# A block-wise seven-product matmul in a float32 decoder layer: another order of the products, other transfers for the weight sums of the last quarter, and one multiply on another engine

## The chip, the cores and the metric

The kernel runs on one core of one Trainium2 chip. The metric is the device time of one execution in microseconds (us). Three runs of the kernel before are shown with a median of 873.74 us.

## What is computed

The reference is one layer of a decoder trunk over 512 tokens of width 1024, in float32: an RMSNorm, one wide input projection, three token mixers (a gated recurrence, dilated attention, attention into a memory), their gated sum through `w_out`, and then an MLP and a last RMSNorm. The change lies in these last lines alone:

```python
    hm = _rmsnorm(x, g_mlp)
    x = x + jnp.square(jax.nn.relu(hm @ w_mlp_in)) @ w_mlp_out    # 1024 -> 4096 -> 1024
return _rmsnorm(x, g_final)
```

## The kernel before

TensorE has no float32 product of full accuracy here, so each float32 operand is split into a rounded part and a rest: `hi = round(src)` on ScalarE (`whi`, `shi`) and `lo = src - hi` on VectorE (`wlo`, `slo`), and a product is three matmuls, hi·hi, hi·lo and lo·hi. A matmul here has 128x128 stationary and 512 moving columns.

**The MLP** runs in four quarters of 1024 hidden columns each. `in_part` computes 128 hidden columns of a quarter (24 matmuls, lines 200 to 202, `mm3`), `hidden` squares their relu into `sq`. The second MLP product of a quarter, 512 x 1024 x 1024, is done by `Product7`: activations and weights are taken as 2x2 blocks (a11 to a22, b11 to b22) and seven products p1 to p7 of block sums replace eight. A weight block is 512x512 floats, 1 MB, in a tile `wq` (one buffer per block, tags `wq00` to `wq11`). `STEPS` gives the order of the seven products, for each the PSUM bank (x, y or z), whether it opens the bank, which quarter of the residual `x2` the bank is then added to, and the sign. In the order before, p1, p2, p5, p6, p7, p4, p3, each product is two parts of 12 matmuls (lines 1118 to 1120): `prep` makes the sums of blocks, `stationary` splits the activation, `split` splits one half of the weight block, `multiply` issues the matmuls and `add` adds the bank to `x2` on VectorE.

**Order of the work.** The list `parts` strings the products and the `in_part`s of the next quarter together; quarters 0 to 2 have `in_part`s between their products, the last quarter (q = 3) has none. The last loop multiplies part i and then splits part i+4, so splits run four parts ahead (four buffers each of `whi` and `wlo`). Within that, each engine has one queue that is worked off in order; the tile framework sets the final order.

**Weight sums.** p5, p6, p7 and p4 take sums of weight blocks (b11+b12, b11+b12+b22 and b12+b22, and all four). In quarters 0 to 2 VectorE adds them in place (128x2048, `V.tensor_add` in `prep`). In the last quarter (`queue` true) they are made by accumulating transfers (`accumulate`: a DMA from GpSimd's queue that adds w_mlp_out's block onto a tile), into `wq01`, `wq00` and a third tile `t2` (`load_sum`, in a `raw` buffer); t2 is used by p6 and, after one more block was added to it, by p4. `free` issues the loads of the next quarter's blocks when a product no longer needs the buffer (`FREE`), on SyncE's queue; `LOADS` is their order for the first quarter.

**The end.** `add` calls `final` for p2, p7, p4 and p3, with which a 128x512 half of `x2` is complete. The first half of a token tile: ScalarE sums its squares, GpSimd multiplies it by `g_final` (line 1157). The second half: ScalarE squares it into the output tile `hnx` (two buffers), VectorE adds the sums, GpSimd raises to the power -0.5 (`rsf`), ScalarE and VectorE scale the two halves, and SyncE sends them out (lines 1171, 1174). A third tile thus needs the buffer of the first, which is free when both of its transfers have landed. The last product is cut for token tile e = 1 into two pieces of 256 columns.

Of the kernel before, what the change touches and what calls it, by code (L numbers as in the profile page):

```python
# [17 lines left out]
P = 128  # L18
# [121 lines left out]
def hybrid_block(ctx: ExitStack, tc: tile.TileContext, x, mem, g_mix, w_in, b_gate, conv_w, conv_b,  # L140
# [856 lines left out]
    class Product7:  # L997
# [14 lines left out]
        def load(self, kh, nh):  # L1012
            b = self.b[kh, nh] = ml.tile([P, 4, 512], F32, name="wq", tag=f"wq{kh}{nh}")
            nc.sync.dma_start(b, self.block(kh, nh))
            if self.queue and (kh, nh) == (0, 1):
                self.accumulate(b, 1, 1)
# [4 lines left out]
        def load_sum(self):  # L1021

            self.t2 = raw_tile(4, 512)
            nc.sync.dma_start(self.t2, self.block(0, 0))
            self.accumulate(self.t2, 0, 1)
            self.accumulate(self.t2, 1, 1)
# [17 lines left out]
        def prep(self, p, sq):  # L1044
# [8 lines left out]
            if p == 5:  # L1053
                self.u = self.sums()
                V.tensor_sub(self.u, a21, a22)
                if not self.queue:
                    V.tensor_add(b11, b11, b12)
# [14 lines left out]
            elif p == 4:  # L1072
                if self.queue:
                    b11 = self.t2
                else:
                    V.tensor_add(b11, b11, b21)
                act, w = a22, b11
            elif p == 3:
                V.tensor_add(self.u, self.u, a12)
                act, w = self.u, b22  # L1080
            else:
                act, w = a12, b21
# [4 lines left out]
        STEPS = ((1, "x", True, (0, 0), 1), (2, "y", True, (0, 0), 1), (5, "z", True, (1, 1), 1),  # L1087
                 (6, "x", False, (0, 1), -1), (7, "x", False, (1, 1), -1), (4, "x", False, (1, 0), 1),
                 (3, "z", False, (0, 1), 1))

        def parts(self, n, sq, done, free):
# [6 lines left out]
            def split(kh):  # L1098
# [4 lines left out]
                if kh == 1:  # L1103
                    free(p)
                    if self.queue and p == 1:
                        self.accumulate(self.b[0, 0], 0, 1)
                    if self.queue and p == 6:
                        self.accumulate(self.t2, 1, 0)
# [40 lines left out]
    def final(t, nh, c0, c1):  # L1149

        v = x2[t][:, nh * 512 + c0:nh * 512 + c1]
        if t not in ss0:
# [4 lines left out]
            G.tensor_tensor(v, v, gbf[:, nh * 512:(nh + 1) * 512], op=ALU.mult)  # L1157
# [37 lines left out]
    def in_part(q, n):  # L1195
        now = {}

        def split():
            m, e = q * 4 + n // 2, n % 2
            now["w"] = split_w(raws[m][:, :, e * P:(e + 1) * P], KT, P)  # L1200
            if e == 1:
                load_in(m + 2)
                if m == 14:
                    prods[3].load_sum()
# [10 lines left out]
    LOADS = ((0, 0), (1, 0), (0, 1), (1, 1))  # L1215
# [4 lines left out]
    for q in range(4):  # L1220
        def free(p, q=q):
            for b in FREE.get(p, ()) if q < 3 else ():
                prods[q + 1].load(*b)
# [50 lines left out]
```

## Time and profile before

| | |
|---|---|
| median of 3 runs (lowest, highest) | 873.74 us (873.71, 875.11) |
| the profiled execution: its time, its span | 873.91 us, 872.1 us |
| TensorE busy | 852.6 us, 98% of the span |
| VectorE, ScalarE, GpSimd busy | 546.9 us (63%), 388.2 us (45%), 31.9 us (4%) |
| mean granted TensorE clock | 0.994 of full speed |

The sum of the prediction is made against the profiled execution, whose time is 0.17 us above the median; 1.8 us of it lie outside the span. A wait is idle time of an engine put down to what released it. Times in the timeline are us from the start of the span. The last quarter begins at about 817 us.

### The profile page before, as it was taken

The page shows a single profiled execution, that of the slowest core. Times are in us where ns is not written, and L with a number is a line of the kernel's source. Part 1 is how long each engine was busy: PE and PEld are TensorE (multiplying, and loading weights), DVE is VectorE, ACT ScalarE, POOL GpSimd, SP SyncE. Part 2 cuts the span into 40 slices and gives each one's busy share as a digit, 9 for nine tenths or more (in the row PEclk, how much of TensorE's full clock was granted, in tenths as well). Part 3 has the DMA queues.
Part 4 walks back from the last instruction along what each step waited for, and adds up shares of the span by engine and source line. Part 5 has one row for each costly group of instructions (what it writes and reads, how often), then busy time and mean ns, then how long its engine had stood idle before and what let it go on. Part 6 is the DMA issues. An engine that isn't in the chain of part 4 may idle for free.

```text
span 872.1 us, 10543 instructions
## 1 busy us (share of the span) xinstructions
PE 852.6 (98%) x4275; PEld 714.6 (82%) x4275; DVE 546.9 (63%) x695; ACT 388.2 (45%) x586; POOL 31.9 (4%) x39
## 2 busy tenths in 40 slices
PE   8999999999999999999999999999999999999975
PEld 7789888889888888888888889888888888888864
DVE  5787766754679642542524446488669757866685
ACT  5467656754635522332332234344425434344444
POOL 2010000000000000000000000000000000001022
PEclk9999999999999999999999999999999999999989
DMA  8862233334322132242325426412431442229422
GB/s 247 265 205 77 68 97 97 97 103 140 114 87 91 49 121 72 82 136 73 101 73 193 141 96 222 141 49 95 147 96 49 145 145 69 76 96 230 108 49 97
DMA packets 82332, 101.16 MB, mean 116 GB/s; under 512 B 3707, under 2 KB 64199, under 8 KB 82156
## 3 DMA queue, kind: packets, MB, share of 16 engines
q1 hardware_dynamic: 78316, 89.03, 32.1%
q0 software_dynamic: 3696, 10.77, 5.4%
q8 instruction: 33, 0.54, 0.3%
q10 hardware_dynamic: 272, 0.69, 0.2%
q14 instruction: 15, 0.12, 0.0%
HBM read 97.32 MB, written 5.52 MB: 118 GB/s over the span
## 4 chain that ended last, share of the span: by engine, by line
PE 85%; DVE 6%; DMA 4%; ACT 2%; issue 2%; POOL 0%; SPq 0%; POOLq 0%; ACTq 0%
PE ps L200 18%; PE ps L202 18%; PE ps L201 18%; PE ps L1118 4%; PE ps L1119 4%; PE ps L1120 4%; DMA wq<-in_w_mlp_out_dram 2%; DVE wlo L95 2%; PE ps L954 2%; PE ps L953 2%; PE ps L952 2%; PE ps L526 1%; PE ps L527 1%; PE ps L528 1%; DMA raw<-in_w_in_dram 1%
## 5 line engine op out<-in xcount | busy, mean ns | idle before, releaser
L95 DVE TENSOR_TENSOR wlo<-raw,whi 128x1024 fp32r<-128x1024 f32 (+1 forms) x125 | 147.7, 1187 | 151.9 <-ACT whi L95 147.6
L95 ACT ACTIVATE whi<-raw 128x1024 fp32r<-128x1024 f32 (+1 forms) x126 | 129.8, 1032 | 222.4 <-PE ps L201 163.6
L200 PE MATMUL ps<-hT_hi,whi 128*128 128x512 f32 x400 | 156.8, 392 | 0.1
L202 PE MATMUL ps<-hT_hi,wlo 128*128 128x512 f32 x400 | 155.6, 390 | 0.4 <-DVE wlo L95 0.4
L201 PE MATMUL ps<-hT_lo,whi 128*128 128x512 f32 x400 | 155.8, 390 | 0.0
L95 DVE TENSOR_TENSOR wlo<-wq,whi 128x1024 fp32r<-128x1024 f32 x52 | 65.4, 1258 | 59.7 <-ACT whi L95 59.7
L95 ACT ACTIVATE whi<-wq 128x1024 fp32r<-128x1024 f32 x52 | 55.0, 1060 | 102.5 <-PE ps L201 51.3
L1118 PE MATMUL ps<-whi,shi 128*128 128x512 f32 (+1 forms) x228 | 89.2, 391 | 5.8 <-DVE x L95 5.8
L201 PE MATMUL ps<-hmT_lo,whi 128*128 128x512 f32 x240 | 93.4, 389 | 0.0
L202 PE MATMUL ps<-hmT_hi,wlo 128*128 128x512 f32 x240 | 93.4, 389 | 0.0
L200 PE MATMUL ps<-hmT_hi,whi 128*128 128x512 f32 x240 | 93.2, 389 | 0.0
L1119 PE MATMUL ps<-wlo,shi 128*128 128x512 f32 (+1 forms) x228 | 88.8, 390 | 0.0
L200 PEld LDWEIGHTS ps<-hT_hi,whi 128*128 128x128 f32 x400 | 75.1, 188 | 16.7 <-issue 0.6
L202 PEld LDWEIGHTS ps<-hT_hi,wlo 128*128 128x128 f32 x400 | 75.1, 188 | 16.4 <-DVE wlo L95 0.8
L1120 PE MATMUL ps<-whi,slo 128*128 128x512 f32 (+1 forms) x228 | 88.4, 388 | 0.0
L201 PEld LDWEIGHTS ps<-hT_lo,whi 128*128 128x128 f32 x400 | 75.1, 188 | 15.1
L1118 PEld LDWEIGHTS ps<-whi,shi 128*128 128x128 f32 x228 | 43.5, 191 | 15.8 <-issue 4.9
L202 PEld LDWEIGHTS ps<-hmT_hi,wlo 128*128 128x128 f32 x240 | 45.1, 188 | 9.4
L201 PEld LDWEIGHTS ps<-hmT_lo,whi 128*128 128x128 f32 x240 | 45.1, 188 | 9.2
L200 PEld LDWEIGHTS ps<-hmT_hi,whi 128*128 128x128 f32 x240 | 45.0, 188 | 9.3
L1120 PEld LDWEIGHTS ps<-whi,slo 128*128 128x128 f32 x228 | 43.3, 190 | 8.8
L1119 PEld LDWEIGHTS ps<-wlo,shi 128*128 128x128 f32 x228 | 43.4, 190 | 8.6
(253 smaller groups left out, 1344.0 us busy)
## 6 DMA issues: line engine op xcount, KB each, us to landing
raw<-in_w_in_dram SPq DMA_DIRECT2D x23, 1024.0 KB, 5.4
raw<-in_w_mlp_in_dram SPq DMA_DIRECT2D x16, 1024.0 KB, 5.8
wq<-in_w_mlp_out_dram SPq DMA_DIRECT2D x16, 1024.0 KB, 6.8
raw<-in_w_in_dram SPq DMA_DIRECT2D x12, 512.0 KB, 5.2
raw<-in_w_mem_kv_dram SPq DMA_DIRECT2D x4, 1024.0 KB, 5.2
raw<-in_w_out_dram SPq DMA_DIRECT2D x4, 1024.0 KB, 5.0
x<-in_x_dram SPq DMA_DIRECT2D x7, 512.0 KB, 4.3
raw<-in_w_lru_out_dram SPq DMA_DIRECT2D x4, 768.0 KB, 4.5
```

The source lines that it names most:

```text
L95: r = fn(*a, **k)
L200: PE.matmul(ps, whi[:, k0 + k, :], ah, start=k == 0, stop=False)
L201: PE.matmul(ps, whi[:, k0 + k, :], al, start=False, stop=False)
L202: PE.matmul(ps, wlo[:, k0 + k, :], ah, start=False, stop=k == nk - 1)
L526: PE.matmul(ps[:, 0:256], ah, hi[:, k % 4, :], start=k == 0, stop=False)
L527: PE.matmul(ps[:, 0:256], ah, lo[:, k % 4, :], start=False, stop=False)
L952: PE.matmul(ps, ah[:, sl], hi[:, k % 2, :], start=k == 0, stop=False)
L953: PE.matmul(ps, ah[:, sl], lo[:, k % 2, :], start=False, stop=False)
L954: PE.matmul(ps, al[:, sl], hi[:, k % 2, :], start=False, stop=k == KT - 1)
L1118: PE.matmul(o, ah[:, k, sl], hi, start=opens and k == 0, stop=False, **more)
L1119: PE.matmul(o, ah[:, k, sl], lo, start=False, stop=False, **more)
L1120: PE.matmul(o, al[:, k, sl], hi, start=False, stop=k == 3, **more)
```

## The change

It changes five things. (1) `STEPS`: the products are done in the order p1, p5, p6, p2, p7, p3, p4, in all four quarters, and `LOADS` follows. (2) In the last quarter b11+b12 for p5 is added by VectorE as in the others; b11 lies in a `raw` buffer that is loaded earlier. (3) The sum of three for p6 (`t2`) is made in a buffer of the `sq` tiles, which is free when p7 of the third quarter is split (`load_sum3`: one load, two accumulating transfers). (4) The sum of four for p4 (`t4`) is made in `wq00` by a copy of t2 from SBUF to SBUF on GpSimd's queue and one accumulating transfer (`load_sum4`); b12+b22 for p7 is accumulated in `wq01` after VectorE has read b12. (5) The multiply by `g_final` goes from GpSimd to VectorE.

```diff
--- before.py
+++ after.py
@@ -1009,21 +1009,24 @@
 
             return cols(self.w, nh * 512, 512, self.k0 + kh * 4, 4)
 
-        def load(self, kh, nh):
-            b = self.b[kh, nh] = ml.tile([P, 4, 512], F32, name="wq", tag=f"wq{kh}{nh}")
+        def load(self, kh, nh, dst=None):
+            b = self.b[kh, nh] = dst or ml.tile([P, 4, 512], F32, name="wq", tag=f"wq{kh}{nh}")
             nc.sync.dma_start(b, self.block(kh, nh))
-            if self.queue and (kh, nh) == (0, 1):
-                self.accumulate(b, 1, 1)
 
         def accumulate(self, dst, kh, nh):
             nc.gpsimd.dma_start(out=dst, in_=self.block(kh, nh), accum_op=ALU.add)
 
-        def load_sum(self):
-
-            self.t2 = raw_tile(4, 512)
-            nc.sync.dma_start(self.t2, self.block(0, 0))
-            self.accumulate(self.t2, 0, 1)
-            self.accumulate(self.t2, 1, 1)
+        def load_sum3(self, dst):
+
+            self.t2 = dst
+            nc.sync.dma_start(dst, self.block(0, 0))
+            self.accumulate(dst, 0, 1)
+            self.accumulate(dst, 1, 1)
+
+        def load_sum4(self):
+            self.t4 = ml.tile([P, 4, 512], F32, name="wq", tag="wq00")
+            nc.gpsimd.dma_start(self.t4, self.t2)
+            self.accumulate(self.t4, 1, 0)
 
         def stationary(self, src):
             i, self.n = self.n, self.n + 1
@@ -1053,8 +1056,9 @@
             if p == 5:
                 self.u = self.sums()
                 V.tensor_sub(self.u, a21, a22)
-                if not self.queue:
-                    V.tensor_add(b11, b11, b12)
+                V.tensor_add(b11, b11, b12)
+                if self.queue:
+                    self.accumulate(b12, 1, 1)
                 act, w = self.u, b11
             elif p == 6:
                 u, self.u = self.u, self.sums()
@@ -1071,7 +1075,7 @@
                 act, w = a11, b12
             elif p == 4:
                 if self.queue:
-                    b11 = self.t2
+                    b11 = self.t4
                 else:
                     V.tensor_add(b11, b11, b21)
                 act, w = a22, b11
@@ -1084,9 +1088,9 @@
             return w
 
 
-        STEPS = ((1, "x", True, (0, 0), 1), (2, "y", True, (0, 0), 1), (5, "z", True, (1, 1), 1),
-                 (6, "x", False, (0, 1), -1), (7, "x", False, (1, 1), -1), (4, "x", False, (1, 0), 1),
-                 (3, "z", False, (0, 1), 1))
+        STEPS = ((1, "x", True, (0, 0), 1), (5, "z", True, (1, 1), 1), (6, "x", False, (0, 1), -1),
+                 (2, "y", True, (0, 0), 1), (7, "x", False, (1, 1), -1), (3, "z", False, (0, 1), 1),
+                 (4, "x", False, (1, 0), 1))
 
         def parts(self, n, sq, done, free):
 
@@ -1102,10 +1106,6 @@
                 now[kh] = split_w(now["w"][:, 2 * kh:2 * kh + 2, :], 2, 512)
                 if kh == 1:
                     free(p)
-                    if self.queue and p == 1:
-                        self.accumulate(self.b[0, 0], 0, 1)
-                    if self.queue and p == 6:
-                        self.accumulate(self.t2, 1, 0)
 
             def mult(e, kh, c0, c1):
                 (ah, al), (whi, wlo) = now["a"], now[kh]
@@ -1154,7 +1154,7 @@
             jk = ep.tile([P, 512], F32, name="jk", tag="hnx", bufs=2)
             A.activation(jk, v, AF.Square, accum_out=ss0[t])
             V.tensor_scalar(ss0[t], ss0[t], 1.0 / D, EPS, op0=ALU.mult, op1=ALU.add)
-            G.tensor_tensor(v, v, gbf[:, nh * 512:(nh + 1) * 512], op=ALU.mult)
+            V.tensor_mul(v, v, gbf[:, nh * 512:(nh + 1) * 512])
             return
         if c0 == 0:
             outs[t] = ep.tile([P, D], F32, name="hnx", bufs=2)
@@ -1201,7 +1201,7 @@
             if e == 1:
                 load_in(m + 2)
                 if m == 14:
-                    prods[3].load_sum()
+                    prods[3].load(0, 0, raw_tile(4, 512))
 
         def multiply():
             ps = psum()
@@ -1212,15 +1212,21 @@
 
         return now, split, multiply
 
-    LOADS = ((0, 0), (1, 0), (0, 1), (1, 1))
+    LOADS = ((0, 0), (0, 1), (1, 1), (1, 0))
     FREE = {7: ((0, 1),), 4: ((0, 0), (1, 0)), 3: ((1, 1),)}
 
 
     parts = [in_part(0, n)[1:] for n in range(2, 8)]
     for q in range(4):
         def free(p, q=q):
+            if q == 2 and p == 7:
+
+                prods[3].load_sum3(ml.tile([P, 4, 512], F32, name="wx", tag="sq", bufs=4))
             for b in FREE.get(p, ()) if q < 3 else ():
-                prods[q + 1].load(*b)
+                if q == 2 and b == (0, 0):
+                    prods[3].load_sum4()
+                else:
+                    prods[q + 1].load(*b)
 
 
         tiles = (2, 2, 1, 1, 1, 1, 0) if q == 2 else (1, 1, 1, 1, 1, 1, 2) if q < 2 else (0,) * 7
```

**GpSimd's queue, from the last norm of the MLP's input on.** `raw_6069` is t2, `wq_6127` is b12 (`wq01`), `wq_6200` b11 (`wq00`). Before:

```order
L1019 DMA raw_6069<-in_w_mlp_out_dram 128x4x512
L1019 DMA wq_6127<-in_w_mlp_out_dram 128x4x512
L1019 DMA raw_6069<-in_w_mlp_out_dram 128x4x512
L1019 DMA wq_6200<-in_w_mlp_out_dram 128x4x512
L95 TENSOR_TENSOR x2_4027<-x2_4027,gbf_4364 128x512
L1019 DMA raw_6069<-in_w_mlp_out_dram 128x4x512
L95 TENSOR_TENSOR x2_4029<-x2_4029,gbf_4364 128x512
L95 TENSOR_TENSOR x2_4031<-x2_4031,gbf_4364 128x512
L95 TENSOR_TENSOR x2_4033<-x2_4033,gbf_4364 128x512
L95 TENSOR_TENSOR rsf_6614<-ss0_2_6570,nhalf_81 128x1
```

After: `wx_6125` is t2, `wq_6273` t4, `wq_6129` b12.

```order
L95 TENSOR_TENSOR rs_4342<-ms_4340,nhalf_81 128x1
L1017 DMA wx_6125<-in_w_mlp_out_dram 128x4x512 x2
L1028 DMA wq_6273<-wx_6125 128x2048
L1017 DMA wq_6273<-in_w_mlp_out_dram 128x4x512
L1017 DMA wq_6129<-in_w_mlp_out_dram 128x4x512
L95 TENSOR_TENSOR rsf_6616<-ss0_0_6524,nhalf_81 128x1
L95 TENSOR_TENSOR rsf_6633<-ss0_1_6536,nhalf_81 128x1
```

The two accumulations for t2 now lead, the copy and the one for t4 follow, the one for p7's operand comes last, and the four multiplies by `gbf` (g_final on all partitions) are gone from between the transfers.

**VectorE's queue, at the turn to the last quarter**, from the second half of p1's weights on. Before: `wq_6202` is p2's weights, `wq_6200` p5's.

```order
L95 TENSOR_TENSOR wlo_6327<-wq_6200,whi_6325 128x1024
L95 TENSOR_TENSOR sq_6098<-sq_6098 128x512
L95 TENSOR_TENSOR u_6382<-sq_5881,sq_6098 128x1024
L95 TENSOR_TENSOR wlo_6348<-wq_6202,whi_6346 128x1024
L95 TENSOR_TENSOR x2_4027<-x2_4027,ps_6033 128x512
L95 TENSOR_TENSOR x2_4029<-x2_4029,ps_6034 128x512
L95 TENSOR_TENSOR slo_6385<-u_6382,shi_6384 128x1024
L95 TENSOR_TENSOR slo_6343<-sq_6098,shi_6342 128x1024
L95 TENSOR_TENSOR wlo_6366<-wq_6202,whi_6364 128x1024
L95 TENSOR_TENSOR wlo_6390<-wq_6200,whi_6388 128x1024
```

After: `raw_6067` is p1's weights and then, with b12 (`wq_6129`) added, p5's; `wx_6125` is p6's.

```order
L95 TENSOR_TENSOR wlo_6329<-raw_6067,whi_6327 128x1024
L95 TENSOR_TENSOR sq_6094<-sq_6094 128x512
L95 TENSOR_TENSOR raw_6067<-raw_6067,wq_6129 128x2048
L95 TENSOR_TENSOR u_6343<-sq_5884,sq_6094 128x1024
L95 TENSOR_TENSOR x2_4031<-x2_4031,ps_5816 128x512
L95 TENSOR_TENSOR wlo_6353<-raw_6067,whi_6351 128x1024
L95 TENSOR_TENSOR x2_4033<-x2_4033,ps_5817 128x512
L95 TENSOR_TENSOR slo_6348<-u_6343,shi_6347 128x1024
L95 TENSOR_TENSOR wlo_6371<-raw_6067,whi_6369 128x1024
L95 TENSOR_TENSOR u_6387<-u_6343,sq_5884 128x1024
L95 TENSOR_TENSOR wlo_6395<-wx_6125,whi_6393 128x1024
```

A 128x2048 add came in, and p5's and p6's rows stand where p2's and p5's did.

**VectorE's queue, ahead of p7**, the fifth product of the last quarter in both orders. Its first matmul waits for the add of p6's bank, `ps_6368` before and `ps_6373` after. Before, from the adds of p2's bank on:

```order
L95 TENSOR_TENSOR x2_4027<-x2_4027,ps_6410 128x512
L95 TENSOR_TENSOR x2_4029<-x2_4029,ps_6411 128x512
L95 TENSOR_TENSOR wlo_6460<-raw_6069,whi_6458 128x1024
L95 TENSOR_SCALAR ss0_0_6441<-ss0_0_6441 128x1
L95 TENSOR_TENSOR slo_6479<-sq_5881,shi_6478 128x1024
L95 TENSOR_SCALAR ss0_1_6453<-ss0_1_6453 128x1
L95 TENSOR_TENSOR wlo_6484<-wq_6127,whi_6482 128x1024
L95 TENSOR_TENSOR x2_4031<-x2_4031,ps_6463 128x512
L95 TENSOR_TENSOR x2_4033<-x2_4033,ps_6464 128x512
L95 TENSOR_TENSOR wlo_6502<-wq_6127,whi_6500 128x1024
L95 TENSOR_TENSOR slo_6517<-sq_6098,shi_6516 128x1024
L95 TENSOR_TENSOR x2_4027<-x2_4027,ps_6368 128x512
```

After, from the adds of p5's bank on:

```order
L95 TENSOR_TENSOR x2_4031<-x2_4031,ps_6415 128x512
L95 TENSOR_TENSOR x2_4033<-x2_4033,ps_6416 128x512
L95 TENSOR_TENSOR wlo_6453<-wq_6276,whi_6451 128x1024
L95 TENSOR_TENSOR sq_5884<-sq_5884 128x4x256
L95 TENSOR_TENSOR wlo_6474<-wq_6129,whi_6472 128x1024
L95 TENSOR_TENSOR x2_4027<-x2_4027,ps_6373 128x512
L95 TENSOR_TENSOR slo_6469<-sq_5884,shi_6468 128x1024
L95 TENSOR_TENSOR x2_4029<-x2_4029,ps_6374 128x512
L95 TENSOR_TENSOR wlo_6492<-wq_6129,whi_6490 128x1024
L95 TENSOR_TENSOR u_6387<-u_6387,sq_6094 128x1024
L95 TENSOR_TENSOR wlo_6515<-wq_6201,whi_6513 128x1024
L95 TENSOR_TENSOR x2_4027<-x2_4027,ps_6494 128x512
```

Before, the add onto `x2_4027` out of p6's bank is the last row shown and follows p7's and p4's splits; after, it stands six rows higher, ahead of p7's second half.

## Rows read from the trace of the kernel before

**Rows 1.** The page's first part: busy us, share of span, instructions of each engine.

```profile
PE 852.6 (98%) x4275; PEld 714.6 (82%) x4275; DVE 546.9 (63%) x695; ACT 388.2 (45%) x586; POOL 31.9 (4%) x39
```

**Rows 2.** Waits of PE: engine line, waited for: us in total, times, longest.

```profile
PE ps L1118 <- DVE x L95: 5.8, 2, 4.5
```

**Rows 3.** Timeline of PE, last quarter: start us, us, what, count [idle before, releaser].

```profile
817.33 0.39 PE L1118 MATMUL ps<-whi,shi 128*128 128x512 f32 x1
...
843.71 0.77 PE L1118 MATMUL ps<-whi,shi 128*128 128x512 f32 x1 [4.46 <-DVE x L95]
...
848.86 0.40 PE L1118 MATMUL ps<-whi,shi 128*128 128x512 f32 x1
...
862.99 0.39 PE L1118 MATMUL ps<-whi,shi 128*128 128x256 f32 x1 [1.35 <-DVE x L95]
...
864.41 0.28 PE L1120 MATMUL ps<-whi,slo 128*128 128x256 f32 x1
```

**Rows 4.** Windows: stretch, us, busy us (instructions) by engine, PEclk, DMA share, GB/s.

```profile
844.00:845.00 1.00, 1.00 (x3) 0.82 (x3) 0.00 (x0) 0.56 (x1) 0.00 (x0) 0.50 0.00 0
```

**Rows 5.** Timeline of VectorE, 774 to 843 us.

```profile
774.78 2.28 DVE L95 TENSOR_TENSOR wq<-wq 128x2048 f32<-128x2048 f32 x1
...
805.02 1.23 DVE L95 TENSOR_TENSOR wlo<-wq,whi 128x1024 fp32r<-128x1024 f32 x1 [1.12 <-ACT whi L95]
...
812.96 1.23 DVE L95 TENSOR_TENSOR wlo<-wq,whi 128x1024 fp32r<-128x1024 f32 x1 [2.93 <-ACT whi L95]
...
814.82 1.22 DVE L95 TENSOR_TENSOR u<-sq 128x1024 f32<-128x1024 f32 x1
...
824.14 1.23 DVE L95 TENSOR_TENSOR wlo<-wq,whi 128x1024 fp32r<-128x1024 f32 x1 [2.37 <-ACT whi L95]
825.29 1.28 DVE L95 TENSOR_TENSOR x<-x,ps 128x512 f32<-128x512 f32 x2
826.48 1.22 DVE L95 TENSOR_TENSOR wlo<-wq,whi 128x1024 fp32r<-128x1024 f32 x1
...
834.68 2.26 DVE L95 TENSOR_TENSOR slo<-sq,shi 128x1024 fp32r<-128x1024 f32 x1
...
836.92 2.58 DVE L95 TENSOR_TENSOR wlo<-wq,whi 128x1024 fp32r<-128x1024 f32 x1
...
842.89 0.68 DVE L95 TENSOR_TENSOR x<-x,ps 128x512 f32<-128x512 f32 x1
```

**Rows 6.** Timeline of GpSimd (POOL): accumulating transfers' issues (L1019) and the multiplies.

```profile
786.86 1.35 POOL L1019 DMA_DIRECT2D raw<-in_w_mlp_out_dram  x1 [256.17 <-DMA raw<-in_w_mlp_out_dram]
...
814.48 1.27 POOL L1019 DMA_DIRECT2D wq<-in_w_mlp_out_dram  x1 [17.49 <-DVE wlo L95]
833.81 2.04 POOL L95 TENSOR_TENSOR x<-x,gbf 128x512 f32<-128x512 f32 x1 [18.05 <-ACT jk L95]
...
836.62 1.79 POOL L95 TENSOR_TENSOR x<-x,gbf 128x512 f32<-128x512 f32 x1
```

**Rows 7.** Timeline of SyncE's queue: a load for the third quarter, t2's load.

```profile
713.86 0.37 SPq L1014 DMA_DIRECT2D wq<-in_w_mlp_out_dram  x1
...
778.23 0.37 SPq L1024 DMA_DIRECT2D raw<-in_w_mlp_out_dram  x1
```

**Rows 8.** Timeline of ScalarE: p1's weights, third quarter; third tile's squares.

```profile
722.33 1.06 ACT L95 ACTIVATE whi<-wq 128x1024 fp32r<-128x1024 f32 x1 [1.40 <-PE ps L1120]
...
862.69 0.63 ACT L95 ACTIVATE hnx<-x 128x512 f32<-128x512 f32 x1 [0.71 <-DVE x L95]
```

**Rows 9.** Issue to landing of the five accumulating transfers (line 1019).

```profile
DMA to landing us min/median/max: 8.5/8.6/13.4
```

**Rows 10.** DMA issues: count, KB each, median us to landing.

```profile
raw<-in_w_out_dram SPq DMA_DIRECT2D x4, 1024.0 KB, 5.0
```

**Rows 11.** Issue to landing of the four second output halves (line 1174).

```profile
DMA to landing us min/median/max: 2.6/2.6/2.6
```

**Rows 12.** Timeline of VectorE, the last output half.

```profile
866.75 0.75 DVE L95 SCALAR_TENSOR_TENSOR hnx<-x,rsf,gbf 128x512 f32<-128x512 f32 x1 [0.66 <-POOL rsf L95]
```

## The prediction

> **What bounds the kernel now.** The page's first part comes first: TensorE is busy 98% of the span [rows 1], so time can only be won where it waits or runs slowly. The waits of PE name the one place of size: matmuls of line 1118 wait 5.8 us in two pieces for an add onto `x2` on VectorE [rows 2]. The timeline of PE puts the longer piece, 4.46 us, at 843.71, the start of p7 in the last quarter, and the shorter, 1.35 us, at 862.99, between the two pieces of the last product [rows 3]. The window behind the stall shows the third loss: a granted clock of 0.50, the 1.2 GHz level, after the engine had been idle [rows 4]. From 843.71 to 848.86 twelve matmuls went by at that level [rows 3]. At full clock p1 to p6 of this quarter, 96 matmuls from 817.33 to about 839.1, took 0.2267 us each, so twelve take 2.72 us and the slow clock cost 5.15 - 2.72 = 2.4 us.
>
> Why was VectorE late? Its timeline is unbroken from 824.14 to 842.89 [rows 5]. Three things put the add at 842.89. The split of p5's weights began at 824.14, after 2.37 us idle behind ScalarE, which waited for the accumulating transfer issued at 814.48, after p1's split [rows 5, 6]. Two subtractions took 2.26 and 2.58 us where their like takes 1.22, while GpSimd multiplied by g_final [rows 5, 6]: 1.04 + 1.36 = 2.4 us. And p5, p6 and p7, each with a subtraction or addition of activations more than p2, came one behind the other. The place that counts is therefore VectorE's queue in the last quarter, then the transfers that feed it, then the end behind the last matmul.
>
> **The change, part by part.**
>
> *Quarters 0 to 2.* The same sums and splits are done in another order; nothing is added. New is that b11 is loaded last, at the slot of the load at 713.86 [rows 7]. With even the slowest landing of an accumulation, 13.4 us [rows 9], it is there at 727.3; ScalarE reads it at 722.33 [rows 8], so it could be 5 us late, but p1's matmuls start 15 blocks of 5.44 us ahead of 817.33, at 735.7. Cost 0; the cover is the four parts of lead, and without it the 5 us would show.
>
> *VectorE in the last quarter.* Steps from start to start are 1.15 us for 128x1024, 0.6 for 128x512 (825.29 to 826.48 for two) and 2.28 for the 128x2048 add [rows 5]. I walk the queue of the changed kernel from p1's second split, which waits for the same slot as before, 812.96. Up to the add that lets p4, now last, start in its first bank there are 22 of 1024, 14 of 512 (the first two multiplies by g_final among them), one of 2048 and two tiny ones: 25.3 + 8.4 + 2.3 + 0.1 = 36.1, and about 0.6 of waiting for ScalarE's squares, which stand behind p4's first split. It ends at 849.7. PE without a stall starts p4 at 817.33 + 6 x 5.44 = 850.0: on time by 0.3 us. Ahead of it: p5's rest is split at 821.7 for a matmul at 823.2; p6's at 827.5 for 828.7; p7's at 837.3 for 839.5; p3's at 843.1 for 845.0. The new 2048 add (2.3 us) is paid by the idle 2.37 us that goes, as p5's weights are no longer behind a transfer. The four multiplies cost VectorE 4 x 0.6 = 2.4 us, where the slowed subtractions cost it 2.4: even. So PE has no stall before p4 and gains 4.6 us at p7 (839.1 to 843.71) and 2.4 of slow clock. The wait between the last product's two pieces stays, some 0.7 us shorter: VectorE reaches the add of the first piece at 854.5, PE goes on at 855.0 and ends at 856.6, against 864.41 + 0.28 = 864.7 [rows 3]. With gaps of 0.4 us in all that follow the stall in the trace, PE wins 8.1 us.
>
> *The transfers.* t2's load stands behind b11's, at about 778.2 plus one issue; before, a load issued at 778.23 beside another let an accumulation start at 786.86 [rows 6, 7]. Two accumulations in series, 8.6 us each at the median, 13.4 at the slowest [rows 9]: landed at 804.5 to 814; p6 asks for it at 820. The copy to `wq00` must wait for p4's last split in the third quarter, 805.02 + 1.23 = 806.3 [rows 5]. No row shows a copy from SBUF to SBUF. It lies between 5.0 us, the quickest 1 MB load [rows 10], and 13.4; I take 8.6, the median of its own queue [rows 9]: 814.9. The last accumulation, p7's b12+b22, is queued behind the copy's landing (t4's accumulation waits for it, in order) and needs VectorE's 2048 add, done at 817.0. Issued there, it lands 8.6 to 13.4 us later: 825.6 to 830.4. VectorE wants p7's split at 834.2, ScalarE so at 833.1. 3 us to spare, hidden behind p6 and p2. With one slow link (t2 at 814, a copy of 13.4 or an accumulation of 13.4) it lands by 832.5, with two at 834 to 837, with all three at 842. t4 is wanted at 842.3 and lands by 824 to 836.
>
> *The end.* Here part is given back. The third token tile squares into the buffer that the first leaves, so it waits for the first's transfers. VectorE gets to p3's adds at 852.7 behind p7's two multiplies; square, power and scaling end at 856.0; the second half is sent at 856.4 and lands 2.6 us later [rows 11], 859.0. In the trace the third tile's squares start at 862.69 [rows 8], there held by an add, and from them to the last scaling at 866.75 [rows 12] and the end it takes what it takes: the code is the same. So the end moves by 862.69 - 859.05 = 3.6 us, and 8.1 - 3.6 = 4.5 us become a new wait.
>
> Sum: 873.91 - 3.64 = 870.27 us against the profiled execution; against the median, which is 0.17 lower, 870.1.
>
> **The rivals.**
>
> *A, the end doesn't hold.* If the buffer wait were hidden, the end would follow the last add: piece two at 857.9, then 2 us to the last scaling, 859.4 to 859.9 instead of 866.75, 866.6 us in all. For it: PE's 8.1 us. Against: two buffers, four tiles, in the code.
>
> *B, one late transfer.* Each us that p7's operand lands after 833.1 costs about one, less the 0.3 of slack. At 835 it costs 1.6, 871.7; at 837.2 the gain is gone, 874. For it: three links in one queue, and a landing of 13.4 when others ran beside [rows 9]. Against: here only two run together.
>
> *C, slower: the copy is far dearer than any row,* some 20 us. The accumulation behind it is issued at 827.6 and lands at 836.2 to 841. At 841 the split is 7.9 us late, p7 stands still for over 5 us, and after a stall like that (4.46 in the trace) the clock falls and costs up to 2.4 more: 7.6 + 2.4 - 3.6 = 6.4 us slower at the worst, 880, and 877 in the middle. It is decided by p7's operand landing after about 838.5. For it: the queue is served in order and the copy's price is unseen.
>
> The Trainium skill has a rule of this kind on its page "SBUF — State Buffer", section on the two separate sides of SBUF: while VectorE holds the port pair that it shares with GpSimd, GpSimd cannot write the descriptors of its transfers. The mechanism as the rows price it, called D: were each of the five issues held up by a VectorE instruction of 1.22 to 2.28 us, the chain would be 6 to 11 us later, p7's operand at 832 to 841, and the time 870 to 878, 873 in the middle. Against it: the issue at 814.48 took 1.27 us with a 1.22 us instruction of VectorE running from 814.82, and the one at 786.86 took 1.35 [rows 5, 6]; both show no such hold, so it gets little. The page ties that rule to VectorE's two-port modes and names a float32 copy; none runs beside these issues, so the trace doesn't contradict it.
>
> **How the numbers follow.** About 0.2%, 1.75 us, is what a measurement of this kernel can tell from no change. The forecast, no stall of over a us, gets 0.66, with its own range 868.9 to 871.7 (steps of VectorE uncertain by 0.03 us over 38, and ScalarE's squares). A gets 0.07, B 0.14 (spread over 871.7 to 875), C 0.09, D 0.04. Faster by over 0.2%, below 872.0: the forecast, A, and 0.02 of B and D, 0.75. Slower, above 875.5: C, all but its mild end, and the late ends of B and D, 0.10. Between: 0.15. The range, 868.0 to 874.2, leaves out A, C and the ends of B and D, under 0.2.
>
> **What would show it.** In the changed profile PE has no idle piece of over 1 us from 817 to 850 and a clock of 1.00 there; VectorE's subtractions are all near 1.22; the 2048 add stands near 815; the copy lands before 820 and the last accumulation before 833; PE ends near 856.6, and ScalarE's square for the third tile waits for a transfer until 859. A stall at p7 with ScalarE waiting for `wq` is B, C or D, told apart by the copy's landing and the length of the issues. A stall at p5, p6 or p3 says my walk of VectorE is wrong.

## The result and the profile after

The changed kernel took 869.24 us (median of 4 runs, 869.07 to 871.28), the kernel before 874.42 beside it; the ratio is 0.9947 (95% interval 0.9935 to 0.9959), by which the gain is 4.6 us. The prediction was 870.1 with a range of 868.0 to 874.2. The profiled execution took 869.25 us with a span of 867.5, so 4.6 us less span than before, where the sum of the prediction gave 3.6.

The page's first part and the waits of PE of the changed kernel (engine line waited for: us in total, times, longest):

```profile
PE 849.6 (98%) x4275; PEld 713.1 (82%) x4275; DVE 548.0 (63%) x700; ACT 388.8 (45%) x586; POOL 23.6 (3%) x35
```

```profile
PE ps L1118 <- DVE x L95: 0.5, 1, 0.5
```

The busy time of TensorE fell by 3.0 us against [rows 1], though it does the same 4275 matmuls: most of it is the slow clock behind the stall, which the prediction priced at 2.4 us. The wait for adds onto `x2`, 5.8 us in two pieces [rows 2], is one piece of 0.5. The timeline of PE shows where it is, and the window that showed the 1.2 GHz level before [rows 4] now shows full clock:

```profile
854.68 0.38 PE L1118 MATMUL ps<-whi,shi 128*128 128x256 f32 x1 [0.51 <-DVE x L95]
```

```profile
844.00:845.00 1.00, 1.00 (x6) 0.84 (x5) 1.00 (x2) 0.84 (x3) 0.00 (x0) 1.00 0.00 0
```

VectorE's timeline through the last quarter (start us, us, operation, count [idle before, releaser]), to be read beside [rows 5]:

```profile
814.59 2.28 DVE L95 TENSOR_TENSOR raw<-raw,wq 128x2048 f32<-128x2048 f32 x1
...
820.25 1.22 DVE L95 TENSOR_TENSOR slo<-u,shi 128x1024 fp32r<-128x1024 f32 x1
...
826.00 1.22 DVE L95 TENSOR_TENSOR slo<-u,shi 128x1024 fp32r<-128x1024 f32 x1
...
835.83 1.23 DVE L95 TENSOR_TENSOR slo<-sq,shi 128x1024 fp32r<-128x1024 f32 x1
...
841.94 1.22 DVE L95 TENSOR_TENSOR slo<-u,shi 128x1024 fp32r<-128x1024 f32 x1 [0.28 <-ACT shi L95]
...
848.41 1.28 DVE L95 TENSOR_TENSOR x<-x,ps 128x512 f32<-128x512 f32 x2
...
862.25 0.75 DVE L95 SCALAR_TENSOR_TENSOR hnx<-x,rsf,gbf 128x512 f32<-128x512 f32 x1 [0.66 <-POOL rsf L95]
```

The five transfers that GpSimd issues, and the landing times (us, lowest, median, highest) of the copy (L1028) and of the accumulations (L1017):

```profile
785.41 1.35 POOL L1017 DMA_DIRECT2D wx<-in_w_mlp_out_dram  x1 [254.82 <-DVE x L95]
795.73 1.30 POOL L1017 DMA_DIRECT2D wx<-in_w_mlp_out_dram  x1 [8.97 <-DMA wx<-in_w_mlp_out_dram]
808.10 0.57 POOL L1028 DMA_DIRECT2D wq<-wx  x1 [11.07 <-DVE x L95]
812.93 1.28 POOL L1017 DMA_DIRECT2D wq<-in_w_mlp_out_dram  x1 [4.26 <-DMA wq<-wx]
817.41 1.27 POOL L1017 DMA_DIRECT2D wq<-in_w_mlp_out_dram  x1 [3.20 <-PE ps L1120]
```

```profile
DMA to landing us min/median/max: 4.5/4.5/4.5
```

```profile
DMA to landing us min/median/max: 8.5/9.6/11.8
```

The last two accumulations end by 826: the profile's DMA share is 1.12 from 817 to 825, 0.94 in the window from 825 and 0.02 in the window from 826. ScalarE took p7's weights when TensorE let it, not a transfer, and the third tile's squares did wait for one (timeline of ScalarE):

```profile
831.02 1.06 ACT L95 ACTIVATE whi<-wq 128x1024 fp32r<-128x1024 f32 x1 [1.60 <-PE ps L1120]
...
858.31 0.63 ACT L95 ACTIVATE hnx<-x 128x512 f32<-128x512 f32 x1 [1.41 <-DMA out_dram<-hnx]
```

**Where the time went, by the last quarter alone.** TensorE runs 180 matmuls from p1's first to the end. Counting back from the last one gives the quarter's start in each trace; the span's end less that start is the quarter's length, and what the earlier 817 us took drops out of it:

| kernel | ratio to before [95% interval] | span | p1 starts | PE ends | last quarter |
|---|---|---|---|---|---|
| before | | 872.1 | 817.33 | 864.69 | 54.77 |
| changed | 0.9947 [0.9935, 0.9959] | 867.5 | 817.22 | 856.38 | 50.28 |
| multiply alone | 1.0045 [1.0031, 1.0059] | 877.0 | 818.98 | 868.46 | 58.02 |
| old transfers | 1.0017 [1.0006, 1.0029] | 872.7 | 816.90 | 864.15 | 55.80 |
| old order | 0.9997 [0.9988, 1.0007] | 873.1 | 818.55 | 865.39 | 54.55 |
| multiply back | 0.9965 [0.9953, 0.9977] | 870.2 | 817.06 | 860.87 | 53.14 |
| back, first pair | 0.9960 [0.9946, 0.9973] | 870.2 | 819.28 | 860.34 | 50.92 |
| back, last pair | 0.9933 [0.9918, 0.9947] | 866.6 | 817.09 | 856.70 | 49.51 |
| b22 twice | 0.9980 [0.9970, 0.9990] | 870.8 | 817.16 | 859.38 | 53.64 |
| b22 three times | 1.0073 [1.0059, 1.0087] | 878.0 | 817.07 | 867.00 | 60.93 |
| own output tiles | 0.9919 [0.9905, 0.9933] | 866.5 | 818.85 | 858.01 | 47.65 |
| own tiles, last pair back | 0.9922 [0.9906, 0.9937] | 864.4 | 817.02 | 856.61 | 47.38 |

Each length is that of one execution; the ratios are of several, but their intervals are some 2 us wide. TensorE ends 8.31 us earlier (864.69 to 856.38), and the tail behind it grew from 7.41 to 11.12 us: 3.71 given back.

### The profile page after: what moved, and what is told of

Read it like the earlier page. It is cut to its first block, busy times and chain, and to the rows that moved or that the text cites. A ratio compares the mean times of both kernels' runs of the same rounds, so it can differ in the third digit from the quotient of the medians.

```text
span 867.5 us, 10536 instructions
## 1 busy us (share of the span) xinstructions
PE 849.6 (98%) x4275; PEld 713.1 (82%) x4275; DVE 548.0 (63%) x700; ACT 388.8 (45%) x586; POOL 23.6 (3%) x35
## 4 chain that ended last, share of the span: by engine, by line
PE 90%; DVE 4%; ACT 2%; DMA 2%; issue 1%; SPq 0%; POOL 0%; POOLq 0%; ACTq 0%
PE ps L200 19%; PE ps L202 19%; PE ps L201 19%; PE ps L1120 5%; PE ps L1118 5%; PE ps L1119 5%; PE ps L952 2%; PE ps L954 2%; PE ps L953 2%; PE ps L526 1%; PE ps L527 1%; PE ps L528 1%; DMA raw<-in_w_in_dram 1%; PE ps L257 1%; PE ps L256 1%
## 5 line engine op out<-in xcount | busy, mean ns | idle before, releaser
L95 DVE TENSOR_TENSOR wlo<-wq,whi 128x1024 fp32r<-128x1024 f32 x50 | 61.0, 1223 | 54.5 <-ACT whi L95 54.5
L95 ACT ACTIVATE whi<-wq 128x1024 fp32r<-128x1024 f32 x50 | 53.0, 1060 | 85.3 <-PE ps L201 36.5
L1118 PE MATMUL ps<-whi,shi 128*128 128x512 f32 (+1 forms) x228 | 87.9, 386 | 0.5 <-DVE x L95 0.5
L1120 PE MATMUL ps<-whi,slo 128*128 128x512 f32 (+1 forms) x228 | 87.8, 385 | 0.0
L1118 PEld LDWEIGHTS ps<-whi,shi 128*128 128x128 f32 x228 | 42.8, 188 | 9.3 <-DVE x L95 0.7
L1120 PEld LDWEIGHTS ps<-whi,slo 128*128 128x128 f32 x228 | 42.8, 188 | 8.5
```

Source lines behind the costliest of these rows:

```text
L95: r = fn(*a, **k)
L1118: PE.matmul(o, ah[:, k, sl], hi, start=opens and k == 0, stop=False, **more)
L1120: PE.matmul(o, al[:, k, sl], hi, start=False, stop=k == 3, **more)
```

## The experiments

### One part of the change at a time

The kernel before with the multiply alone, and the changed kernel with the other two parts undone in turn.

```diff
-            G.tensor_tensor(v, v, gbf[:, nh * 512:(nh + 1) * 512], op=ALU.mult)
+            V.tensor_mul(v, v, gbf[:, nh * 512:(nh + 1) * 512])
```

> The kernel before, with the multiply by g_final alone put on VectorE. Theory Q (VectorE's queue: the time is won because the add of p6's bank comes in time for p7, which needs the order, the transfers and the multiply together) expects nothing won here: the subtractions go back to 1.22 us each (2.4 us won), but four multiplies of some 0.6 us come into the same queue, and in the program's order for VectorE the add of p6's bank now stands behind the first split of p4's weights, which waits for the third accumulation on t2 (issued near 834.7, landing 8.6 us later, 843.3). p7 starts near 845.7 instead of 843.71, and the time is 875 to 876.5 us, the kernel before 873.9. Rival M (the gain is the multiply's leaving GpSimd, which frees VectorE's subtractions): 870 to 872.

Measured: 1.0045, 3.3 us longer in the last quarter. PE's row below is the first of p7; then come the split of p4's weights on ScalarE, and on VectorE the rest of that split and the adds of p6's bank.

```profile
848.26 0.76 PE L1118 MATMUL ps<-whi,shi 128*128 128x512 f32 x1 [7.36 <-DVE x L95]
```

```profile
845.21 2.00 ACT L95 ACTIVATE whi<-raw 128x1024 fp32r<-128x1024 f32 x2 [6.51 <-DMA raw<-in_w_mlp_out_dram]
```

```profile
846.30 1.23 DVE L95 TENSOR_TENSOR wlo<-raw,whi 128x1024 fp32r<-128x1024 f32 x1 [2.97 <-ACT whi L95]
847.44 1.28 DVE L95 TENSOR_TENSOR x<-x,ps 128x512 f32<-128x512 f32 x2
```

The stall is 7.36 us where it was 4.46 [rows 3]: the add of p6's bank now stands behind a split that a transfer holds. The mechanism is the one expected, the size above the range by 0.7 us in the quarter and by 1.3 in the ratio. The subtractions are back at 1.22 us, and that wins nothing: rival M falls for this order.

```diff
-        STEPS = ((1, "x", True, (0, 0), 1), (5, "z", True, (1, 1), 1), (6, "x", False, (0, 1), -1),
+        STEPS = ((1, "x", True, (0, 0), 1), (2, "y", True, (0, 0), 1), (5, "z", True, (1, 1), 1),
...
-    LOADS = ((0, 0), (0, 1), (1, 1), (1, 0))
+    LOADS = ((0, 0), (1, 0), (0, 1), (1, 1))
```

> The changed kernel with the order of the products of the kernel before (p1, p2, p5, p6, p7, p4, p3), the new transfers and the multiply on VectorE. Theory Q: the sums are there in time, but p5, p6 and p7 stand one behind the other in VectorE's queue again, and the new 2048 add is in it too: the add of p6's bank ends near 843, p7 starts there after a stall of about 4 us and a slow clock, 872 to 874 us. Rival T (the earlier transfers bring the gain): 869 to 870.

Measured: 0.9997, the time of the kernel before, and so at the upper end of what theory Q gave. p7 starts behind a stall of 4.27 us, with all its operands there; the adds onto `x2` that it waits for come out of a VectorE queue that has had one gap, of 0.29 us, since 814.18:

```profile
844.75 0.77 PE L1118 MATMUL ps<-whi,shi 128*128 128x512 f32 x1 [4.27 <-DVE x L95]
```

```profile
843.92 1.28 DVE L95 TENSOR_TENSOR x<-x,ps 128x512 f32<-128x512 f32 x2
```

Transfers and multiply without the order bring nothing; rival T falls.

```diff
-            self.t2 = dst
-            nc.sync.dma_start(dst, self.block(0, 0))
...
+            self.t2 = raw_tile(4, 512)
+            nc.sync.dma_start(self.t2, self.block(0, 0))
...
-                V.tensor_add(b11, b11, b12)
+                if not self.queue:
+                    V.tensor_add(b11, b11, b12)
...
+                    if self.queue and p == 1:
+                        self.accumulate(self.b[0, 0], 0, 1)
```

> The new order of the products and the multiply on VectorE, with the weight sums of the last quarter made by the transfers of the kernel before. Theory Q: p5 now follows p1 at once, but its weights wait for the accumulation that is issued after p1's split (near 815.5, landing near 824). Its second split follows at 826 or so, p5 is late by 2.5 to 3.5 us, with a slow clock behind it; p7 has no stall, and the time is 872 to 874.5 us. Rival O (the order alone brings the gain, the transfers are hidden anyway): 869 to 870.

Measured: 1.0017, 1.0 us longer in the last quarter than before, so over what theory Q gave by 0.4 us in the quarter and by 0.9 in the ratio. The stall is at p5 as told and p7 has none, but it is 4.93 us, and the accumulation is issued at 817.61, not 815.5:

```profile
827.44 0.80 PE L1118 MATMUL ps<-whi,shi 128*128 128x512 f32 x1 [4.93 <-ACT whi L95]
```

```profile
813.86 2.01 ACT L95 ACTIVATE whi<-wq 128x1024 fp32r<-128x1024 f32 x2 [9.30 <-DMA wq<-in_w_mlp_out_dram]
...
826.33 2.00 ACT L95 ACTIVATE whi<-wq 128x1024 fp32r<-128x1024 f32 x2 [4.33 <-DMA wq<-in_w_mlp_out_dram]
```

What the expectation left out is the first row: with p4 last, b11's buffer comes free later, p1's own split waits for its load until 813.86, and the accumulation behind it slides too. The changed kernel's b11 in a `raw` buffer is what avoids both rows. Rival O falls: with the multiply on VectorE, the order without the transfers or the transfers without the order win nothing, and both 4.5 us. Order alone or transfers alone with the multiply left on GpSimd was not run.

### The multiply, back on GpSimd

The reverse of the edit above in the changed kernel, for all four tiles.

> The changed kernel, with the multiply by g_final put back on GpSimd. Theory Q: no stall before p4 comes back, since two slowed subtractions (2.4 us) stand against four multiplies that leave VectorE's queue (2.4 us); some idle time of up to 1 us at p4 and at its second piece, 869.5 to 871, the changed kernel 869.2. Rival M: the slowed subtractions are the loss that was won, so at least half of the gain goes, 872 or more.

Measured: 0.9965, 1.6 us over the changed kernel by the ratios (their intervals just overlap), in theory Q's range, but 2.86 by the last quarter, over it. The stall ahead of p4 is small as theory Q says (0.16 us), but the second piece is dearer than it told, and by the time, 872, the rival would be right; the rows tell whose mechanism it is. PE, VectorE and GpSimd of this kernel:

```profile
850.02 0.47 PE L1118 MATMUL ps<-whi,shi 128*128 128x512 f32 x1 [0.16 <-DVE x L95]
...
857.94 0.58 PE L1118 MATMUL ps<-whi,shi 128*128 128x256 f32 x1 [3.44 <-DVE x L95]
```

```profile
843.59 2.33 DVE L95 TENSOR_TENSOR wlo<-wq,whi 128x1024 fp32r<-128x1024 f32 x1
...
845.90 2.24 DVE L95 TENSOR_TENSOR slo<-sq,shi 128x1024 fp32r<-128x1024 f32 x1
...
849.21 1.27 DVE L95 TENSOR_TENSOR x<-x,ps 128x512 f32<-128x512 f32 x2
...
850.40 1.21 DVE L95 TENSOR_TENSOR wlo<-wq,whi 128x1024 fp32r<-128x1024 f32 x1
...
856.21 0.75 DVE L95 SCALAR_TENSOR_TENSOR hnx<-x,rsf,gbf 128x512 f32<-128x512 f32 x1 [0.66 <-POOL rsf L95]
856.87 1.01 DVE L95 TENSOR_TENSOR x<-x,ps 128x512 f32<-128x512 f32 x2
```

```profile
843.54 3.52 POOL L95 TENSOR_TENSOR x<-x,gbf 128x512 f32<-128x512 f32 x2 [25.03 <-ACT jk L95]
850.77 3.25 POOL L95 TENSOR_TENSOR x<-x,gbf 128x512 f32<-128x512 f32 x2 [3.71 <-ACT jk L95]
854.12 0.56 POOL L95 TENSOR_TENSOR rsf<-ss,nhalf 128x1 f32<-128x1 f32 x1
```

The power (`rsf`) follows the second pair of multiplies at once, the scalings wait for the power, and the adds that TensorE waits for stand behind the scalings at 856.87: 3.44 us of idle time, and then the slow clock:

```profile
858.00:859.00 1.00, 1.00 (x5) 1.00 (x6) 0.00 (x0) 0.65 (x2) 0.00 (x0) 0.50 1.00 381
```

To see which pair does it, each was put back alone.

```diff
-            V.tensor_mul(v, v, gbf[:, nh * 512:(nh + 1) * 512])
+            if len(ss0) <= 2:
+                G.tensor_tensor(v, v, gbf[:, nh * 512:(nh + 1) * 512], op=ALU.mult)
+            else:
+                V.tensor_mul(v, v, gbf[:, nh * 512:(nh + 1) * 512])
```

> The changed kernel, with the multiply by g_final back on GpSimd for the first two token tiles alone (those whose half p2 and p7 complete first in the last quarter), where all four together cost 2.86 us in the last quarter. Theory V (VectorE's queue ahead of p4): two subtractions go from 1.22 to about 2.3 us, 2.2 us more, and two multiplies of 0.6 us leave VectorE, so the adds that p4 and the first tiles' squares wait for come 1.0 us later, and with them the first scaling and the output transfers that hold the third tile: 0.7 to 1.1 us over the changed kernel in the last quarter, 50.28 us there. Rival W (the whole cost lies in the power on GpSimd waiting for the last two multiplies): 0 to 0.3 us.

> The changed kernel, with the multiply back on GpSimd for the last two token tiles alone. Theory V: the multiplies on GpSimd run from about 850.3 to 853.6, the first tile's power follows at 853.7 to 854.2, where it stands in the changed kernel too, so the scaling and its transfers stay; the add that the last product's second piece waits for goes behind that scaling, up to 1.5 us of idle time on TensorE, covered by the third tile's wait: 0 to 0.4 us over the changed kernel. The 2.86 us of all four then come only with both pairs, since the first pair's delay pushes the second pair in front of the power. Rival W: 2 to 2.9 us.

Measured (the second has `> 2` in place of `<= 2`): 50.92 and 49.51 us, 0.64 more and 0.77 less than the changed kernel, both under what theory V gave (0.7 to 1.1, and 0 to 0.4). Rival W falls: the last pair alone costs nothing, by the quarter or by the ratio. The first pair, which slows the subtractions, costs 0.64 us by the quarter and 1.1 by the ratio, so rival M's mechanism is there but is not half of the gain. That both pairs together cost more than their sum rests on one execution of each; by the ratios, both pairs (0.9965) and the first alone (0.9960) can't be told apart. The last pair is even a small gain in the last quarter: its multiplies run beside adds that read PSUM, the subtraction ahead of them keeps its time, and the power is ready at 853.76 where the changed kernel has it at 854.66:

```profile
849.48 1.22 DVE L95 TENSOR_TENSOR wlo<-wq,whi 128x1024 fp32r<-128x1024 f32 x1
```

```profile
849.87 3.24 POOL L95 TENSOR_TENSOR x<-x,gbf 128x512 f32<-128x512 f32 x2 [31.31 <-ACT jk L95]
853.20 0.56 POOL L95 TENSOR_TENSOR rsf<-ss,nhalf 128x1 f32<-128x1 f32 x1
```

By the ratios this kernel and the changed one can't be told apart (the intervals overlap).

### How late p7's operand may come

```diff
                     self.accumulate(b12, 1, 1)
+                    self.accumulate(b12, 1, 1)
```

> The changed kernel, with the block that is accumulated onto p7's weights accumulated twice, one after the other: b12 + 2 b22 in place of b12 + b22 in the last quarter, a transfer's length added to the queue. Theory Q: the second is issued when the first has landed, near 826, and lands near 834.5; the prediction has p7's operand wanted by 833.1 and about one us of time for each us after that, less 0.3: 0 to 1.5 us over the changed kernel, 869.2 to 870.8. Rival S (the transfers share the DMA engines without waiting for each other, or the slack at p7 is larger than told): no change, 869.2, with the last landing before 830 or a p7 without any idle time though it landed after 834. Rival U (p7's operand is already just in time in the changed kernel): 8 us over, 876 to 878.

> The changed kernel, with that block accumulated three times: b12 + 3 b22 in place of b12 + b22 in the last quarter. Theory Q: the last lands near 843, ten us after p7's operand is wanted; ScalarE's split follows at once and p7 starts near 844.3 to 845.5, 5 to 6 us late, with 2.4 us of slow clock: 5 to 9 us over the changed kernel, 874.5 to 878.5. Rival S: 869.2 to 870.

Measured: 53.64 and 60.93 us, 3.4 and 10.7 over the changed kernel. With two, GpSimd issues the second at 826.60 and ScalarE starts p7's split when it has landed:

```profile
826.60 1.28 POOL L1017 DMA_DIRECT2D wq<-in_w_mlp_out_dram  x1 [7.98 <-DMA wq<-in_w_mlp_out_dram]
```

```profile
836.50 2.01 ACT L95 ACTIVATE whi<-wq 128x1024 fp32r<-128x1024 f32 x2 [7.14 <-DMA wq<-in_w_mlp_out_dram]
```

The landing was 2 us later than expected (836.5 for 834.5), so the time missed the expected range, but the rule's size held: 836.5 is 3.4 us after 833.1, less 0.3 of slack is 3.1, and 3.36 were measured. No single stall shows it; TensorE ends 3.06 us later, counted from p1, and falls back by 1.5 us at p7, 0.3 in p3, 1.1 at p4's start and 0.1 at its last piece. With three, the split starts 10.6 us late and the quarter is 10.65 longer, over the 5 to 9 expected; p7 itself stands still for 7.72 us, and the rest is slow clock. The split of p7's weights, and p7's first matmul (two lines were added to this kernel, so L1118 is L1120 here):

```profile
843.66 2.00 ACT L95 ACTIVATE whi<-wq 128x1024 fp32r<-128x1024 f32 x2 [14.38 <-DMA wq<-in_w_mlp_out_dram]
```

```profile
846.72 0.76 PE L1120 MATMUL ps<-whi,shi 128*128 128x512 f32 x1 [7.72 <-ACT shi L95]
```

Rivals S and U fall: a late operand costs about its lateness, and the changed kernel's own is not yet late. But the sum comes out for another reason than the 0.3 us of slack: p7 alone had 2 to 3 us to spare (1.5 lost for 3.4 late, 7.7 for 10.6), and what was lost behind it, to VectorE's late queue at p4 or to the slow clock, makes up for that.

### The wait at the end

```diff
-            outs[t] = ep.tile([P, D], F32, name="hnx", bufs=2)
+            if len(outs) < 2:
+                outs[t] = ep.tile([P, D], F32, name="hnx", bufs=2)
+            else:
+                o4 = ml.tile([P, 4, 512], F32, name="o4", tag=f"wq1{len(outs) - 2}")
+                outs[t] = o4.rearrange("p a b -> p (a b)")[:, 0:D]
```

> The changed kernel, with output tiles of their own for the third and fourth token tile (in weight buffers that are free by then), so that the third tile's squares no longer wait for the first tile's output transfers. Theory E (the end is held by that wait, as the prediction has it): the squares start behind the last adds, near 854.6 instead of 858.31, the last scaling near 858.8 to 859.9 instead of 862.25, and the time falls by 2.4 to 3.5 us to 865.7 to 866.8. Rival F (the wait covers others of the same length, GpSimd's powers, SyncE's queue or the two tiles' squares on ScalarE): 868.5 to 869.3.

Measured: 0.9919 (0.9905 to 0.9933), 2.63 us less in the last quarter, 2.4 by the ratios: theory E, in its range as a difference. The third tile's squares follow the second's at once (ScalarE), and the last add is now held by VectorE's order behind two scalings:

```profile
855.11 0.61 ACT L95 ACTIVATE hnx<-x 128x512 f32<-128x512 f32 x1
...
855.72 0.61 ACT L95 ACTIVATE o<-x 128x512 f32<-128x512 f32 x1
```

```profile
857.81 0.75 DVE L95 SCALAR_TENSOR_TENSOR hnx<-x,rsf,gbf 128x512 f32<-128x512 f32 x1 [0.59 <-POOL rsf L95]
858.48 0.75 DVE L95 SCALAR_TENSOR_TENSOR o<-x,rsf,gbf 128x512 f32<-128x512 f32 x1
...
859.21 0.41 DVE L95 TENSOR_TENSOR x<-x,ps 128x256 f32<-128x256 f32 x1
```

So of the 3.71 us that the tail gave back, the wait for the buffer held 2.63. The last run joins this edit and the multiply of the last pair on GpSimd.

> The two edits that shortened the last quarter together: output tiles of their own for the third and fourth token tile, and the multiply by g_final on GpSimd for the last two token tiles alone. In the kernel with own output tiles the last add (859.21) stood 1.2 us behind TensorE's end (858.01), in VectorE's queue behind two scalings. Theory X (that queue is what is left): the scalings come 0.9 us earlier, TensorE's end some 0.4 us later, the add follows at once, and the last quarter falls from 47.65 to 46.7 to 47.2 us; the ratio to the kernel before is 0.990 to 0.992. Rival Y (the later second piece of the last product, no longer covered by the third tile's wait, costs what the earlier scalings win): 47.4 to 48.0 us, ratio 0.991 to 0.993.

Measured: 0.9922, and 47.38 us in the last quarter, at rival Y's lower end (47.4). The last add still comes 0.7 us after TensorE's end, behind the third tile's scaling, and counted from p1 it stands at 40.33 us where it stood at 40.36 without the multiply's move: what the scalings win, TensorE's end loses (39.59 for 39.16). Both kernels with output tiles of their own are faster than the kernel before. Against the changed one, the interval of the first lies clear below (0.9933 under 0.9935), that of the second overlaps at its end (0.9937); between the two there is nothing to choose.

## Why the prediction was right, step by step

- *What bounds it.* Right. The stall at p7, the slow clock behind it and most of the wait in the last product are gone, and the old order alone brings them back.
- *Quarters 0 to 2, cost 0.* Right: p1 of the last quarter starts at 817.22, before at 817.33.
- *VectorE's walk.* Right to 0.3 us at the four products that it named ahead of p4: p5's rest was split at 821.5 (told 821.7), p6's at 827.2 (827.5), p7's at 837.1 (837.3), p3's at 843.2 (843.1). The add that lets p4 start in its first bank, the first of the two at 848.41, ended at about 849.1, 0.6 earlier than told (849.7): a step took 1.14 us for the 1.15 used, and VectorE waited 0.28 us for the 0.6 allowed. So p4 had more to spare than the 0.3 told, and no stall came before it. The 2048 add stands at 814.59, with 2.28 us, as told.
- *"The four multiplies cost VectorE 4 x 0.6 = 2.4 us, where the slowed subtractions cost it 2.4: even."* Wrong, without harm to the forecast. Ahead of p4 only two of the four multiplies leave VectorE when they are put back (1.2 us), and two subtractions are slowed by 2.1 (2.33 and 2.24 for 1.22): the adds come 1.0 us later, counted from p1 (849.21 less 817.06, for 848.41 less 817.22), and only p4's spare time keeps the stall at 0.16. As a price of the whole edit it is wrong too: putting all four back costs 1.6 us by the ratios and 2.86 by the quarter, through GpSimd's queue to the power, the scalings and the last adds, which the prediction did not follow. And the multiply's sign hangs on the other parts: in the kernel before, with its order and its transfers, the move costs 3.3 us.
- *TensorE's end.* 856.38 for 856.6; 8.3 us won for 8.1. The one idle piece is 0.51 us.
- *The transfers.* t2's second accumulation landed at about 807.5 (795.73 + 11.8; told 804.5 to 814). The copy was mis-sized: 4.5 us for a taken 8.6, and under the lower bound of 5.0. It cost nothing, since p7's accumulation was issued at 817.41 (817.0) and had landed by 826 (825.6 to 830.4) for a demand at 831 to 833. The slope of rival B, a us for each late us, is what the doubled transfer measured as a sum, with more spare time at p7 and more loss behind it than told; rival B itself didn't come to pass.
- *The end.* The mechanism was right, its time a little off, and this makes nearly the whole difference between 870.27 and the profiled execution's 869.25, 0.96 of 1.02 us. The third tile's squares came at 858.31, told 859.05, as p3's adds began at 852.07 for 852.7 and the second half was sent at 855.85 for 856.4. That is 0.74 us. From squares to the last scaling took 3.94 us, before 4.06, and the rest 5.25, before 5.35. So 4.5 us were to be given back and 3.7 were.
- *The rivals.* A ("the buffer wait is hidden") is excluded by ScalarE's row at 858.31. With tiles of their own the kernel does what A told: its last scaling comes 42.24 us after p1's start, 859.5 on the changed kernel's clock (A: 859.4 to 859.9), and its ratio is 7.1 us under the kernel before (A: 873.74 - 866.6 = 7.1). C fell with the copy's 4.5 us. D fell with the issues, 0.57 us for the copy and 1.27 to 1.35 for each accumulation, as in the kernel before, the one at 812.93 beside a subtraction of VectorE from 812.84.

## What to carry to other kernels

Where TensorE is at 98%, walk the queue of the engine that feeds it, instruction by instruction: sums of 1.15 us steps placed four products to 0.3 us and the last to 0.6. Order, transfers and the engine of a small operation are not separate gains, so price each with the others in place: the multiply's move cost 3.3 us alone and won 1.6 to 2.9 beside the other two. And ask what ends last once the stall is gone: the wait for output buffers and what follows it took 3.7 us of 8.3 back, and output tiles of their own for two token tiles fetched 2.6 of them.

## What the runs showed of the hardware

**VectorE and GpSimd take turns.** In the kernel with all four multiplies back, the subtraction at 843.59 began 0.05 us after GpSimd's multiply and took 2.33 us; the one at 850.40 began 0.37 us before the next multiply and took 1.21. Adds out of PSUM beside such multiplies keep their time (1.27 us for two in the last-pair kernel, while its multiplies ran). The Trainium skill has this as a rule on its page "SBUF — State Buffer", section "Who interferes with whom": a VectorE instruction with two SBUF inputs contends with a GpSimd one that reads SBUF, and the pair of ports is an exclusive lock, which whoever starts first holds. These rows agree in who is held up.

**The copy from SBUF to SBUF** took 4.5 us for 1 MB, where the quickest group of loads of that size had a median of 5.0 [rows 10] and the accumulations took 8.5 to 11.8.

**The clock can fall without a stall.** In three of the twelve profiled executions (old order, multiply alone, own output tiles) TensorE ran at the 1.2 GHz level for some 3 us from 270 or 271 us on, though its rows show it busy. Windows of the kernel with own output tiles, then of the changed kernel:

```profile
266.00:276.00 10.00, 10.00 (x44) 7.92 (x43) 8.86 (x16) 2.80 (x4) 0.00 (x0) 0.83 0.01 2
```

```profile
266.00:276.00 10.00, 10.00 (x55) 8.20 (x54) 9.22 (x17) 3.52 (x7) 0.00 (x0) 1.00 0.01 2
```

What TensorE did just before is eight matmuls over 4 partitions in place of 128 (lines 728 and 729); the last of them in the kernel with own output tiles, and the first slow one behind it:

```profile
269.59 0.38 PE L729 MATMUL ps<-cfl,hs 4*128 4x512 f32 x1
269.90 0.65 PE L200 MATMUL ps<-hT_hi,whi 128*128 128x512 f32 x1
```

The changed kernel does the same eight there and keeps its clock, so what decides is open. In these three, p1 of the last quarter starts 1.3 to 1.8 us later than in the changed kernel (818.55 to 818.98 for 817.22). In a fourth late one, with the first pair back (819.28), the clock was low in the first 20 us already (0.83, and 0.91 in the multiply alone, where the changed kernel has 1.00). That is why the quarter's length, and not the span, was compared.
